# Two gate stages that scale and squash both halves of a block before the rest, and narrow weights loaded into a small tile

## The chip, the cores and the metric

The kernel runs on one core of a Trainium2 chip. The metric is the device time of one execution in microseconds (us); below 0.2% (5.6 us) two versions of it cannot be told apart.

## The reference

Two model blocks run one after the other over 1024 positions of width 1024, batch 1, in float32. The first has two layers, one with windowed attention and one with latent attention (`mla`), and each layer ends in a gate; the second has a state-space branch and an attention branch behind one wide projection. What the change touches is, cut to its core:

```python
# first block, per layer i (0: windowed attention, 1: mla)
h = h + y
gate = jax.nn.sigmoid(rms_norm(h, ple_norm_g[i]) @ ple_w_gate[i])     # 1024 x 1024
h = h + (p[i] @ ple_w[i]) * gate
# mla: cq 384 columns, ckv 256, k_rope 32, z 1024
cq, ckv, k_rope, z = jnp.split(u @ w_in, ...)
# second block: ada = silu(c) @ w_ada + b_ada gives shift, scale, gate
h = _rmsnorm(x, norm_w) * (1.0 + scale) + shift
z_ssm, xbc, dt_raw, q, k, v, z_att, f_logit, g_logit = jnp.split(h @ w_in, ...)   # dt_raw 16 columns, f_logit 8
```

## The kernel before, in words

Activations are kept transposed: 8 tiles (k = 0 to 7) of 128 channels by 1024 positions, worked on in two halves of 512 positions. To keep float32 accuracy each operand is split into a high and a low part, and a product takes three matmuls (`mm3`: L148, L149, L150). An output block of 128 channels costs 24 matmuls per half. Its weights come in on a DMA into a raw tile (`wr`, 2 buffers), ScalarE makes the high part (L107), VectorE the low part (L108). Every tile is taken from a ring with a fixed number of buffers: `wr`, `wh`, `wl` have 2, `T` (128x512, for scratch) has 4, `P` has 4, PSUM has two double-half tiles `S` and three single-half `TR`. A new tile waits until the old one in its buffer has been read for the last time.

**The gate, `ple`.** Each block n = 0 to 7 is multiplied and then evacuated half by half: VectorE multiplies PSUM by the norm's factor into a `T` tile (L438), ScalarE applies tanh (L754), VectorE multiplies by the projected embedding (L755) and adds into h (L756), and `nxt` then prepares the next stage: in layer 0 the split of the new h (L88 on ScalarE, L89 on VectorE) and its squares (L311 on ScalarE, L325 on GpSimd, summed over positions by one-column matmuls, L335); in layer 1 the squares of two norms. Layer 0 calls `lin`, which computes both halves and then evacuates both. Layer 1 calls `lin1`: first all blocks of half 0, then of half 1; between them the second norm's factor is worked out, and pieces of `second_in` (L1087 to L1090) are slipped in.

**The ada steps.** In layer 0 each gate block is followed by two steps of `ada_steps`: a 512 KB DMA of a row block of w_adaT into a `P` tile (L1051) and one VectorE reduction over it (L1053).

**Narrow weights, `stacked`.** The 32 columns of k_rope (`mla_in`) and the 16+16 columns for dt and f (`ssd_in`) are loaded into a raw tile (L124), and their high and low parts (L126 on ScalarE, L127 on VectorE) stand side by side in one `wh` tile; `mm2` (L134) multiplies both at once, 16 matmuls per half. In `mla_in` they come after the ckv blocks, in `ssd_in` directly after the last gate block.

The order within each engine's queue is not the order of the code: a scheduler in the framework places the instructions by its own estimates before the kernel is built. At run time each engine works through its queue strictly in that order, so an instruction that waits holds up all that stand behind it.

Of the kernel before, what the change touches and what calls it, by code (L numbers as in the profile page):

```python
# [17 lines left out]
ALU = mybir.AluOpType  # L18
AX = mybir.AxisListType

P = 128
T = 1024
NB = 8
# [15 lines left out]
class Kern:  # L39
# [79 lines left out]
    def stacked(self, srcs):  # L119

        nc = self.nc
        raw = self.t("wr", (P, NB, 32))
        for c, s in srcs:
            nc.sync.dma_start(raw[:, :, c:c + s.shape[1]], s.rearrange("(k p) n -> p k n", p=P))  # L124
        w = self.t("wh", (P, NB, 64), F32R)
        nc.scalar.activation(w[:, :, 0:32], raw, AF.Copy)  # L126
        nc.vector.tensor_tensor(w[:, :, 32:64], raw, w[:, :, 0:32].bitcast(F32), op=ALU.subtract)  # L127
        return w
# [22 lines left out]

    def lin(self, w, x, evac, cut=0, tag="S"):

        if tag == "S":
            ps = self.ps("S", (P, 2, HT))
            ps = [ps[:, half, :] for half in range(2)]
        else:
            ps = [self.ps(tag) for _ in range(2)]
        for k0, k1 in ((0, cut), (cut, len(x))):
            if k0 < k1:  # L160
                for half in range(2):
                    self.mm3(ps[half], w, x, half, k0, k1)
        for half in range(2):
            evac(half, ps[half])

    def lin1(self, w, x, half, evac, tag=None):

# [576 lines left out]
    def ple(self, i, hs, xs, rb, nxt, side):  # L744

        nc = self.nc
        wg = self.A["ple_w_gate"][i]
        pwd = self.pwd

        def evac(n, pw, off):  # L750
            def ev(half, ps):
                sl = slice(half * HT, half * HT + HT)
                t = self.scaled(ps, rb, half)
                nc.scalar.activation(t, t, AF.Tanh, scale=0.5)  # L754
                nc.vector.scalar_tensor_tensor(t, t, 1.0, pw[:, sl] if off is None else pw, op0=ALU.add, op1=ALU.mult)  # L755
                nc.vector.scalar_tensor_tensor(hs[n][:, sl], t, 0.5, hs[n][:, sl], op0=ALU.mult, op1=ALU.add)  # L756
                nxt(n, half, hs[n][:, sl])
            return ev
        if i == 0:
            for n in range(NB):  # L760
                pw = self.t("P")
                nc.sync.dma_start(pw, pwd[n])
                self.lin(self.weights([(0, wg[:, n * P:n * P + P])], NB), xs, evac(n, pw, None), CUT if n == 0 else 0)
                next(side)
                next(side)
            return
        for half in range(2):
            for n in range(NB):
                pw = self.t("P", (P, HT))
                nc.sync.dma_start(pw, pwd[n, :, half * HT:half * HT + HT])  # L770
                self.lin1(self.weights([(0, wg[:, n * P:n * P + P])], NB), xs, half, evac(n, pw, half))
                for _ in range(0 if half == 0 else (1, 1, 1, 2, 2, 2, 0, 0)[n]):
                    next(side)

# [1026 lines left out]
```

## Time and profile before

| what | us |
|---|---|
| median of 3 runs (2803.79 to 2805.35) | 2805.26 |
| the profiled execution, its own time | 2801.53 |
| its span | 2799.8 |
| TensorE (PE) busy | 2730.1 |
| VectorE (DVE) busy | 1614.5 |
| ScalarE (ACT) busy | 1317.6 |
| GpSimd (POOL) busy | 964.1 |

A timeline row gives the start, the duration, the engine, the line, the operation and its tiles, and at its end the time the engine had been idle and whose end let it go. SPq is the queue of DMA issues; its rows are the issue, not the transfer. PEclk is the granted TensorE clock, 1.00 for 2.4 GHz and 0.50 for 1.2 GHz. A row marked x2 or x8 holds that many instructions. A 512-column matmul lasts 0.39 us but starts 0.23 us after the one ahead of it, so 24 take 5.5 us. The gate of layer 0 runs from 527 to 612 us, `mla_in`'s narrow weights stand at 665, the gate of layer 1 runs from 1414 to 1517, and `ssd_in` starts there.

### The profile page before, as it was taken

The numbers are of one execution on the slowest core, as the hardware profiler recorded it, in microseconds if no ns is written. First come the engines' busy times: TensorE is split into PE (matmuls) and PEld (weight loads), VectorE is DVE, ScalarE is ACT, GpSimd is POOL, SyncE is SP. The second block draws the span as 40 slices with busy tenths as digits, with TensorE's granted clock in tenths as the row PEclk, the third lists the DMA queues.
The fourth block names the chain that finished last, engine by engine and source line by source line (L and its number), as shares of the span: only waits on it lengthen the run. The fifth ranks groups of instructions, "written<-read, shape, count | busy, mean of one in ns | idle before, by whom it ended". The sixth has DMA issues, their size and how long they took to land.

```text
span 2799.8 us, 37840 instructions
## 1 busy us (share of the span) xinstructions
PE 2730.1 (98%) x13951; PEld 2248.3 (80%) x13951; DVE 1614.5 (58%) x2981; ACT 1317.6 (47%) x2520; POOL 964.1 (34%) x802
## 2 busy tenths in 40 slices
PE   8999989999999999999998999999999999999998
PEld 6888778878888888888876777777888888888877
DVE  6786864565478778876467674564322332323364
ACT  5675663333267777786344444532133333334231
POOL 2333352112145555553234113221144444543031
PEclk9999999999999999999999999999999999999999
DMA  4011034452431111112344111223411111112442
GB/s 141 24 31 46 26 106 158 123 170 52 107 80 34 34 34 39 48 44 81 109 136 133 31 54 50 76 83 106 136 46 46 38 46 38 46 50 91 132 140 79
DMA packets 249304, 212.89 MB, mean 76 GB/s; under 512 B 35296, under 2 KB 203296, under 8 KB 249120
## 3 DMA queue, kind: packets, MB, share of 16 engines
q1 hardware_dynamic: 249120, 210.49, 25.8%
q8 instruction: 110, 1.80, 0.3%
q14 instruction: 74, 0.61, 0.1%
HBM read 159.03 MB, written 38.44 MB: 71 GB/s over the span
## 4 chain that ended last, share of the span: by engine, by line
PE 80%; DVE 9%; ACT 4%; DMA 3%; issue 3%; POOL 1%; SPq 0%; DVEq 0%; ACTq 0%; POOLq 0%
PE psTR L185 9%; PE psTR L187 9%; PE psTR L186 9%; PE psS L149 8%; PE psS L148 8%; PE psS L150 8%; PE psOV L999 4%; PE psTR L988 3%; PE psS L1692 3%; DMA P<-in_w_adaT 2%; PE psS L969 2%; PE psS L971 2%; PE psS L970 2%; PE psTR L1586 1%; PE psOV L650 1%
## 5 line engine op out<-in xcount | busy, mean ns | idle before, releaser
L86 DVE TENSOR_TENSOR PT<-psTR,PT 128x512 fp32r<-128x512 f32 (+2 forms) x448 | 284.5, 646 | 184.8 <-ACT PT L85 182.1
L107 ACT ACTIVATE wh<-wr 128x1024 fp32r<-128x1024 f32 (+2 forms) x185 | 177.1, 958 | 422.0 <-PE psS L149 295.0
L185 PE MATMUL psTR<-X,wh 128*128 128x512 f32 x864 | 354.1, 410 | 3.6 <-DVE PT L86 3.3
L85 ACT ACTIVATE PT<-psTR 128x512 fp32r<-128x512 f32 (+2 forms) x448 | 246.2, 563 | 221.8 <-PE psTR L1586 137.8
L187 PE MATMUL psTR<-X,wl 128*128 128x512 f32 x864 | 342.7, 397 | 0.0
L186 PE MATMUL psTR<-X,wh 128*128 128x512 f32 x864 | 341.1, 395 | 0.0
L108 POOL TENSOR_TENSOR wl<-wr,wh 128x1024 fp32r<-128x1024 f32 x66 | 159.1, 2410 | 393.0 <-ACT wh L107 392.7
L148 PE MATMUL psS<-X,wh 128*128 128x512 f32 x688 | 271.9, 397 | 11.3 <-ACT wh L107 6.9
L149 PE MATMUL psS<-X,wh 128*128 128x512 f32 x688 | 271.9, 396 | 0.6 <-POOL X L676 0.3
L150 PE MATMUL psS<-X,wl 128*128 128x512 f32 x688 | 271.3, 395 | 0.9 <-DVE wl L108 0.9
L325 POOL TENSOR_TENSOR R<-R,T 128x512 f32<-128x512 f32 x81 | 118.5, 1464 | 411.1 <-ACT T L311 381.6
L999 PE MATMUL psOV<-PT,X 128*128 128x256 f32 x1024 | 188.6, 297 | 8.1 <-DVE PT L86 5.5
L187 PEld LDWEIGHTS psTR<-X,wl 128*128 128x128 f32 x864 | 162.7, 188 | 36.4 <-issue 1.7
L185 PEld LDWEIGHTS psTR<-X,wh 128*128 128x128 f32 x864 | 163.4, 189 | 30.2 <-DVE PT L86 4.0
L186 PEld LDWEIGHTS psTR<-X,wh 128*128 128x128 f32 x864 | 163.5, 189 | 23.4 <-issue 0.8
L953 DVE TENSOR_REDUCE nm<-psS 128x1 f32<-128x1024 f32 x128 | 155.5, 1216 | 20.8 <-PE psS L971 20.2
L148 PE MATMUL psS<-G,wh 128*128 128x512 f32 x400 | 159.4, 399 | 7.4 <-ACT wh L107 4.4
L999 PEld LDWEIGHTS psOV<-PT,X 128*128 128x128 f32 x1024 | 147.8, 189 | 22.4 <-DVE PT L86 7.4
L148 PEld LDWEIGHTS psS<-X,wh 128*128 128x128 f32 x688 | 130.7, 190 | 41.9 <-ACT wh L107 8.6
L150 PE MATMUL psS<-G,wl 128*128 128x512 f32 x400 | 159.9, 400 | 0.2 <-DVE wl L108 0.2
L108 DVE TENSOR_TENSOR wl<-wr,wh 128x1024 fp32r<-128x1024 f32 (+2 forms) x93 | 116.6, 1255 | 74.7 <-ACT wh L107 73.9
L149 PE MATMUL psS<-G,wh 128*128 128x512 f32 x400 | 159.3, 398 | 0.0
(414 smaller groups left out, 6473.5 us busy)
## 6 DMA issues: line engine op xcount, KB each, us to landing
wr<-in_w_in SPq DMA_DIRECT2D x66, 512.0 KB
wr<-in_ple_w_gate SPq DMA_DIRECT2D x24, 512.0 KB
wr<-in_a_w_in SPq DMA_DIRECT2D x16, 512.0 KB
P<-in_w_adaT SPq DMA_DIRECT2D x16, 512.0 KB
gd<-T SPq DMA_DIRECT2D x32, 256.0 KB
T<-gd SPq DMA_DIRECT2D x32, 256.0 KB
wr<-in_b_w_in SPq DMA_DIRECT2D x13, 512.0 KB
X<-X SPq DMA_DIRECT2D x48, 128.0 KB
```

The costliest lines, as they stand in the source:

```text
L85: last = nc.scalar.activation(hi, src, AF.Copy)
L86: (nc.gpsimd if pool else nc.vector).tensor_tensor(lo, src, hi.bitcast(F32), op=ALU.subtract)
L107: self.nc.scalar.activation(hi[:, k, :], raw[:, k, :], AF.Copy)
L108: (self.nc.gpsimd if pool else self.nc.vector).tensor_tensor(lo[:, k, :], raw[:, k, :], hi[:, k, :].bitcast(F32), op=ALU.subtract)
L148: self.nc.tensor.matmul(ps, hi[:, k, :], xh, start=(k == 0), stop=False)
L149: self.nc.tensor.matmul(ps, hi[:, k, :], xl, start=False, stop=False)
L150: self.nc.tensor.matmul(ps, lo[:, k, :], xh, start=False, stop=(k == nk - 1))
L185: nc.tensor.matmul(ps, hi[:, k, :], xh, start=(k == 0), stop=False)
L186: nc.tensor.matmul(ps, hi[:, k, :], xl, start=False, stop=False)
L187: nc.tensor.matmul(ps, lo[:, k, :], xh, start=False, stop=(k == nk - 1))
L953: nc.vector.tensor_reduce(nm, st, axis=AX.X, op=ALU.max, negate=True)
L999: nc.tensor.matmul(po[:, u % 2, :], vt[:, 2 * kk + a, :], pe[:, part, a, :], start=(kk + a == 0 and part == 0), stop=(kk + a == 4 and part ...
```

## The change

The raw tile of `stacked` is taken from the ring `T` instead of `wr`. `lin` collects what `evac` returns and calls it after both halves. In `ple` the evacuation ends with tanh and returns the rest as a function. In layer 0 both halves thus pass L438 and tanh before either passes L755. In layer 1 the evacuation of block 0 of half 0 is held back until block 1's matmuls have been emitted; the other blocks are evacuated as before.

```diff
     def stacked(self, srcs):
-        raw = self.t("wr", (P, NB, 32))
+        raw = self.t("T", (P, NB, 32))
...
     def lin(self, w, x, evac, cut=0, tag="S"):
-        for half in range(2):
-            evac(half, ps[half])
+        late = [evac(half, ps[half]) for half in range(2)]
+        for fn in late:
+            if fn is not None:
+                fn()
...
                 t = self.scaled(ps, rb, half)
                 nc.scalar.activation(t, t, AF.Tanh, scale=0.5)
-                nc.vector.scalar_tensor_tensor(t, t, 1.0, pw[:, sl] if off is None else pw, op0=ALU.add, op1=ALU.mult)
-                nc.vector.scalar_tensor_tensor(hs[n][:, sl], t, 0.5, hs[n][:, sl], op0=ALU.mult, op1=ALU.add)
-                nxt(n, half, hs[n][:, sl])
+
+                def rest():
+                    nc.vector.scalar_tensor_tensor(t, t, 1.0, pw[:, sl] if off is None else pw, op0=ALU.add, op1=ALU.mult)
+                    nc.vector.scalar_tensor_tensor(hs[n][:, sl], t, 0.5, hs[n][:, sl], op0=ALU.mult, op1=ALU.add)
+                    nxt(n, half, hs[n][:, sl])
+                return rest
...
+        rest = []
         for half in range(2):
             for n in range(NB):
...
-                self.lin1(self.weights([(0, wg[:, n * P:n * P + P])], NB), xs, half, evac(n, pw, half))
+                rest.append(self.lin1(self.weights([(0, wg[:, n * P:n * P + P])], NB), xs, half,
+                                      lambda half, ps, ev=evac(n, pw, half): lambda: ev(half, ps)()))
+                if half > 0 or n > 0:
+                    for fn in rest:
+                        fn()
+                    rest.clear()
```

The instructions are the same ones; their places in the queues differ in the gate of layer 0, around the narrow weights in `mla_in`, and from the gate of layer 1 into `ssd_in`. Lines of the changed kernel are numbered 3 higher from `lin` on and 12 higher behind `ple` (L438 is L441, L755 is L760, L1053 is L1065).

In the gate of layer 0 this is one block (the sixth, PSUM tile 5642) in VectorE's queue, before:

```order
L438 TENSOR_TENSOR T_5691<-psS_5642,R_5245 128x512
L108 TENSOR_TENSOR wl_5812<-wr_5810,wh_5811 128x1024
L1053 ISA P_5802,ada_552<-P_5802,P_5275,vec_78 128x1024
L1053 ISA ada_552 128x1
L755 SCALAR_TENSOR_TENSOR T_5691<-T_5691,P_5634 128x512
L756 SCALAR_TENSOR_TENSOR O_4939<-T_5691,O_4939 128x512
L438 TENSOR_TENSOR T_5704<-psS_5642,R_5245 128x512
L89 SCALAR_TENSOR_TENSOR X_5697<-O_4939,vec_78,X_5696 128x512
L1053 ISA P_5805,ada_552<-P_5805,P_5275,vec_78 128x1024
```

and now:

```order
L441 TENSOR_TENSOR T_5691<-psS_5642,R_5245 128x512
L441 TENSOR_TENSOR T_5694<-psS_5642,R_5245 128x512
L1065 ISA P_5802,ada_552<-P_5802,P_5275,vec_78 128x1024
L1065 ISA ada_552 128x1
L108 TENSOR_TENSOR wl_5812<-wr_5810,wh_5811 128x1024
L760 SCALAR_TENSOR_TENSOR T_5691<-T_5691,P_5634 128x512
L760 SCALAR_TENSOR_TENSOR T_5694<-T_5694,P_5634 128x512
L761 SCALAR_TENSOR_TENSOR O_4939<-T_5691,O_4939 128x512
L761 SCALAR_TENSOR_TENSOR O_4939<-T_5694,O_4939 128x512
L1065 ISA P_5805,ada_552<-P_5805,P_5275,vec_78 128x1024
```

The second half's read of PSUM has moved ahead of the reduction over w_adaT; the next weights' low part has moved behind it.

The narrow weights of `mla_in` in the queue of DMA issues, before (`wr_6399` and `wr_6464` are later, wide weights):

```order
L104 DMA wr_6170<-in_b_w_in 128x8x128
L776 DMA h2d<-O_5087 128x512 x2
L104 DMA wr_6237<-in_b_w_in 128x8x128
L124 DMA wr_6337<-in_b_w_in 128x8x32
L104 DMA wr_6399<-in_b_w_in 128x8x128
L104 DMA wr_6464<-in_b_w_qb 128x3x32 x4
```

and now:

```order
L104 DMA wr_6237<-in_b_w_in 128x8x128
L104 DMA wr_6399<-in_b_w_in 128x8x128
L104 DMA wr_6464<-in_b_w_qb 128x3x32 x4
L124 DMA T_6337<-in_b_w_in 128x8x32
L104 DMA wr_6514<-in_b_w_in 128x8x128
```

The load has moved behind two wide ones, and its `T` buffer is that of T_6292, the first half of the last ckv block after its scaling: the load waits until L88, L89 and L311 (now L88, L89, L314) have read that. TensorE's queue puts the eight L335 of that block's norm ahead of the 32 L134, where before they came after.

The narrow weights of `ssd_in` in the same queue, before (`h4d<-O` are the stores of the gate's result, half 1, one per block):

```order
L776 DMA h4d<-O_14003 128x512
L124 DMA wr_15217<-in_w_in 128x8x16 x2
L770 DMA P_15119<-pwd_12758 128x512
L776 DMA h4d<-O_14077 128x512
L104 DMA wr_15225<-in_w_in 128x8x128
L770 DMA P_15164<-pwd_12758 128x512
L104 DMA wr_15233<-in_w_in 128x8x128
L776 DMA h4d<-O_14151 128x512
```

and now:

```order
L104 DMA wr_15241<-in_w_in 128x8x128
L777 DMA P_15164<-pwd_12758 128x512
L788 DMA h4d<-O_14151 128x512
L104 DMA wr_15600<-in_w_in 128x8x128
L788 DMA h4d<-O_14225 128x512
L788 DMA h4d<-O_14299 128x512
L124 DMA T_15217<-in_w_in 128x8x16 x2
L104 DMA wr_15666<-in_w_in 128x8x128
```

The load has moved from the fourth of the eight blocks' stores to behind the last; its buffer is that of the squares of block 6, whose last reader is GpSimd's addition (L328, before L325). On ScalarE and VectorE L126 and L127 now stand behind everything of block 7. TensorE's queue still has the 16 L134 next after the last gate block, then the 16 L338 (before L335) and then the first conv block; before, the conv block's matmuls stood between them.

At the middle of layer 1's gate TensorE's queue before had L335 directly behind block 0 of half 1, then blocks 1 and 2; now it has block 2, the L338, and blocks 1, 4, 3. Weights for block 2 take the buffer that block 0 frees, weights for block 4 that of block 1.

## Rows read from the trace of the kernel before

**Rows 1.** The page, parts 1 and 4: busy time by engine, and the chain.

```profile
PE 2730.1 (98%) x13951; PEld 2248.3 (80%) x13951; DVE 1614.5 (58%) x2981; ACT 1317.6 (47%) x2520; POOL 964.1 (34%) x802
...
PE 80%; DVE 9%; ACT 4%; DMA 3%; issue 3%; POOL 1%; SPq 0%; DVEq 0%; ACTq 0%; POOLq 0%
```

**Rows 2.** Windows: length, then PE, PEld, DVE, ACT, POOL busy, PEclk, DMA share, GB/s.

```profile
500.00:620.00 120.00, 113.25 (x497) 90.31 (x496) 79.89 (x118) 42.37 (x64) 22.06 (x16) 1.00 0.52 158
...
1440.00:1480.00 40.00, 36.07 (x151) 29.14 (x150) 30.44 (x53) 17.75 (x26) 18.58 (x14) 0.91 0.55 171
...
1517.00:1574.00 57.00, 51.72 (x219) 39.13 (x219) 35.64 (x69) 25.23 (x38) 20.63 (x14) 0.88 0.27 74
...
1472.30:1479.10 6.80, 6.80 (x24) 5.93 (x24) 5.79 (x30) 1.42 (x3) 0.73 (x1) 0.50 0.39 117
...
1523.50:1530.30 6.80, 4.57 (x10) 2.82 (x11) 5.54 (x8) 3.20 (x5) 0.42 (x1) 0.50 0.37 92
```

**Rows 3.** Timeline of TensorE, gate of layer 0: two of five gaps.

```profile
588.36 0.47 PE L148 MATMUL psS<-G,wh 128*128 128x512 f32 x1 [1.30 <-ACT X L88]
...
612.75 0.50 PE L148 MATMUL psS<-X,wh 128*128 128x512 f32 x1 [2.35 <-ACT X L88]
```

**Rows 4.** Timeline of VectorE, gate of layer 0.

```profile
587.53 0.68 DVE L438 TENSOR_TENSOR T<-psS,R 128x512 f32<-128x512 f32 x1
...
591.43 1.28 DVE L1053 CUSTOM_DVE_ANT_0 P<-P,P,vec 128x1024 f32<-128x1024 f32 x1 [2.27 <-DMA P<-in_w_adaT]
```

**Rows 5.** Timeline of the DMA queue, gate of layer 0.

```profile
580.45 0.33 SPq L1051 DMA_DIRECT2D P<-in_w_adaT  x1
...
586.31 0.33 SPq L1051 DMA_DIRECT2D P<-in_w_adaT  x1
...
593.35 0.33 SPq L1051 DMA_DIRECT2D P<-in_w_adaT  x1
```

**Rows 6.** Timelines of PE, ACT and POOL around mla_in's narrow weights.

```profile
664.87 7.53 PE L134 MATMUL psS<-X,wh 128*64 128x512 f32 x32
...
672.92 1.84 PE L335 MATMUL psTR<-ones,R 128*128 128x1 f32 x16
...
653.97 0.42 ACT L126 ACTIVATE wh<-wr 128x256 fp32r<-128x256 f32 x1 [10.57 <-PE psS L149]
...
665.86 0.71 ACT L88 ACTIVATE G<-T,vec 128x512 fp32r<-128x512 f32 x1
...
667.22 3.14 POOL L325 TENSOR_TENSOR R<-R,T 128x512 f32<-128x512 f32 x2 [21.90 <-ACT T L311]
```

**Rows 7.** Timelines of the DMA queue and POOL: two 64 KB moves and their reader.

```profile
675.78 1.22 SPq L812 DMA_DIRECT2D P<-P  x2
...
679.03 3.25 POOL L813 TENSOR_TENSOR P<-P,PT 32x1024 f32<-32x1024 f32 x1 [8.67 <-DMA P<-P]
```

**Rows 8.** Timelines of PE, ACT and DVE at the middle of layer 1's gate.

```profile
1471.86 1.52 PE L335 MATMUL psTR<-ones,R 128*128 128x1 f32 x8 [3.88 <-POOL R L325]
...
1470.92 1.04 ACT L107 ACTIVATE wh<-wr 128x1024 fp32r<-128x1024 f32 x1
...
1471.99 2.12 DVE L108 TENSOR_TENSOR wl<-wr,wh 128x1024 fp32r<-128x1024 f32 x1 [1.65 <-ACT wh L107]
```

**Rows 9.** Timelines of PE, DVE and POOL, end of the gate and ssd_in.

```profile
1516.84 0.40 PE L150 MATMUL psTR<-G,wl 128*128 128x512 f32 x1
1517.83 2.06 PE L134 MATMUL psTR<-G,wh 128*64 128x512 f32 x8 [0.60 <-DVE wh L127]
...
1525.49 0.79 PE L148 MATMUL psS<-G,wh 128*128 128x512 f32 x1 [4.44 <-ACT wh L107]
...
1574.21 0.40 PE L148 MATMUL psS<-G,wh 128*128 128x512 f32 x1
...
1517.37 0.41 DVE L127 TENSOR_TENSOR wh<-wr,wh 128x256 fp32r<-128x256 f32 x1
...
1532.46 1.74 POOL L325 TENSOR_TENSOR P<-P,T 128x512 f32<-128x512 f32 x1
```

## The prediction

> **What bounds the kernel now.** I read the page first: TensorE (PE) is busy 2730.1 of 2799.8 us and makes up 80% of the chain [rows 1]. So a shorter or longer evacuation counts only where PE stands still for it, or where PE runs at the lower clock. Then windows over the stages that the change touches [rows 2]: in the gate of layer 0 (500 to 620 us) PE is idle 120 - 113.25 = 6.75 us at full clock; from 1440 to 1480, the middle of layer 1's gate, 3.9 us at a mean clock of 0.91; from 1517 to 1574, where ssd_in begins, 5.3 us at 0.88. Last the timelines at these gaps, to see who lets PE go [rows 3 to 9]. About 16 us of idle time and some clock loss is all that any reordering here can win; but PE has no slack, so a wait put into its way is paid in full.
>
> One feature of the clock matters for each wait. After 3.88 us of idle at 1471.86 [rows 8] the granted clock is 0.50 for at least 6.8 us [rows 2]; in the gate of layer 0, whose longest gap is 2.35 us [rows 3], it stays 1.00 [rows 2]. So I charge a stall of 3.5 us or more another 3.4 us (half of 6.8), and one of 2.5 us nothing.
>
> **The gate of layer 0.** Before, PE's start at 588.36 waits [rows 3] for the PSUM tile of two blocks earlier, whose second half L438 reads at 587.53 [rows 4]. (The row names L88, which was long done; L438's end fits.) That L438 stands behind a reduction L1053 which waits for its w_adaT load: issue 586.31, start of the reduction 591.43, thus 5.12 us, after DVE had waited 2.27 [rows 4, 5]. The loads are serial, since each waits for the reduction before it: issues at 580.45, 586.31 and 593.35, 6.45 us each, 12.9 a block, against 11.0 for the block's 48 matmuls at 0.23. So DVE falls behind PE and hands PSUM back late; that is the 6.75 us.
>
> Now L438 of both halves stand ahead of the reduction. The second half's read comes one load earlier (6.4 us) less the 0.7 of its new neighbours, more than the largest gap, so the gaps between blocks go. The loads stay serial; one issue in two no longer has the embedding's load ahead of it and saves 0.6. What takes the gaps' place: L108 of a later block now stands behind the reduction, and would come up to 0.9 late at one block (I take 0.4); the first block of mla_in still wants the split of the last gate block, where the 2.35 gap stood, for which I take 1.2; and 0.4 for the squares. Sum 6.75 - 2.0 = 4.7 saved. Bounds: 6.75, all of it, and 1.5, if the loads pace the weights instead.
>
> **Narrow weights in mla_in.** Before, they lay ready: L126 ran at 653.97 and the 32 L134 at 664.87, with no gap [rows 6]. Now the load waits for the buffer of the ckv block that PE has only just finished at 665.1. Readers of that buffer: L88 at 665.86 for 0.71, then L89 and L311, about 667.3 in all; the load goes out then. The time from issue to use of a 128 KB load in 128-byte pieces stands in no row. Below, two moves of 64 KB each are issued from 675.78 for 1.22 and read at 679.03, so 2.6 us after the last issue [rows 7]; above, 512 KB takes 5.1 [rows 4, 5]. I take 3.0, near the 64 KB row. Then L126 0.42 and L127 0.41 with 0.2 for hand-over: L134 starts at 671.3 instead of 665.1, 6.2 us later. In that gap PE can do the eight L338, whose additions end on POOL at 670.4 [rows 6], worth 1.7 us (672.92 to 674.6 before). Left 4.5 idle, and 3.4 for the clock: 7.9 lost. Bounds: with 2.6 and no clock loss 4.1; with 5.1 and a longer low clock 11.5.
>
> The Trainium skill (DMA: Bandwidth & Descriptors, Anatomy of one DMA) puts a transfer at 2.0 us plus bytes over 436 GB/s, fitted for another issuing engine; an estimate by it is 2.3 us here, and the sum would be 0.7 us smaller at this place and at the next. The rows above, which include the queue, are longer, and I go by them.
>
> **The gate of layer 1.** At its start one more wait for the broadcast of the norm's factor, hidden before behind block 1: 0.3 lost. In the middle, L335 waited 3.88 us for POOL's sum of block 7, with 3.4 for the clock, together 7.3. Now block 2 comes first. Its weights take the buffer that PE has just freed: L107 1.04 and then L108, 2.12 beside POOL's additions [rows 8]; two matmuls run in between, so 2.5 idle. The same once more at block 4, whose weights take block 1's buffer and whose L108 stands third in DVE's queue: 2.6. So 2.2 saved, if neither lowers the clock; bounds 0 and 7.
>
> **Narrow weights in ssd_in.** This is the largest term. Before, PE ends the gate at 1517.1 and starts L134 at 1517.83, as L127 has run at 1517.37 [rows 9]. Now the load waits for POOL's second addition of block 6, which before ended at 1532.46 + 1.74 = 1534.2, 17.1 us after PE's end, because a block's tail passes DVE, ACT and POOL in turn and these are that far behind PE. In the new order one L108 is done earlier and L127 and another L108 later, but PE also ends earlier, so I take 15 us. Then 3.3 for two issues and landing, 0.42 and 0.41 for L126 and L127, 0.2: PE idle for 19.3 us. The L338 that stand next can't run ahead in an ordered queue, nor the conv block behind them. Then the same work as before with one stretch of low clock (3.4) and 1.0 for waits on the second half's activations: 23.7 lost. Before, the losses of this stretch were 0.7 + 5.3 idle, and 0.88 of mean clock over 57 us is 13.7 us at half speed, of which PE was busy 11.4 (2.2 of idle lies in the window at 1523.5 [rows 2]), so 5.7: 11.7 in all. Net 12 lost. Bounds: 4, if POOL is only 8 us behind; 18 with 5.1 for the landing, a longer low clock and POOL as late as before.
>
> **Sum.** -4.7 + 7.9 + 0.3 - 2.2 + 12 = +13.3 us on the profiled execution of 2801.53 (span 2799.8), so 2814.8. The median of the runs, 2805.26, is 3.7 above that execution: 2818.5. A fifth of a percent, 5.6 us, is what a measurement of this kernel can tell from no change.
>
> **Rivals.**
> First, faster: the narrow load hides. `T` turns over in a ring of four, so if its buffer fell free 5 us before PE came, both loads would be covered as before and only the gates' gains stay: -4.7 + 0.3 - 2.2, and up to 4 more where ssd_in's stall of 4.44 [rows 9] shrinks because the wide weights no longer share `wr` with it: 2795 to 2799. It decides at the end of POOL's addition against PE's end of the gate; the trace has that addition 17 us late, and mla_in's buffer is freed only by the block that PE has just finished. 0.08. The Trainium skill (Trainium Kernel Development and Optimization, Best Practices) says to double-buffer so that DMA overlaps compute; by that rule four buffers would give this rival. The trace speaks against it, as the ring here is held by the evacuation itself.
>
> Second, a draw: the gates give all they can (6.75 and 7) and the narrow loads cost their lower bounds (4.1 and about 6): -3.7, 2801 to 2809. For it: the scheduler put the work so by its own estimates. Against: two bounds at once. 0.13.
>
> Third, the loads pace the gate: layer 0 saves 1.5, layer 1 nothing, the two waits take 11.5 and 16: +26, 2831. For it: the serial loads are no fewer than before, and DVE's L108 took 2.12 beside POOL [rows 8]. 0.10.
>
> Fourth, the reordering of halves brings nothing because PE's gaps in layer 0 come from the split L88, as the row says, and not from PSUM: then +4.7 more than forecast, 2823, within the range. 0.09.
>
> **How the numbers follow.** The forecast has 0.60 with its own range of 2811 to 2825. Out to the draw and towards the third rival, 2804 to 2829 holds 8 in 10. Faster by over 5.6 us: the first rival and a part of the draw, 0.10. Within 5.6 us (to 2811): the rest of the draw and the forecast's low end, 0.13. Slower: 0.77.
>
> **What would show it.** In the profile after: no gaps over 1 us between gate blocks of layer 0, with two L441 in a row on DVE; TensorE idle some 5 us just before L134 at about 665, ended by L127, and the granted clock at 0.50 behind it; two gaps of about 2.5 us after block 0 of half 1; and one gap of 15 to 22 us ahead of L134 at the end of the gate, with the load L124 issued when POOL's addition of block 6 ends. The prediction is wrong if that last gap is under 8 us, if L124 is issued before PE ends the gate, or if layer 0 keeps its gaps.

## The result, and the profile after

The changed kernel takes 2830.22 us (median of 4 runs, 2829.02 to 2832.63) against 2805.31 us for the kernel before, run beside it: a ratio of 1.0085, interval 1.0069 to 1.0101. It is slower, as forecast, but by 24.9 us where 13.3 were forecast. That is 5.2 us above the forecast's own range (2811 to 2825) and 1.2 above the wider one (2804 to 2829). The profiled execution took 2829.53 us (span 2827.5). Its page, part 1:

```profile
PE 2732.4 (97%) x13951; PEld 2247.7 (79%) x13951; DVE 1611.8 (57%) x2981; ACT 1317.6 (47%) x2520; POOL 969.6 (34%) x802
```

TensorE has the same 13951 matmuls and 2.3 us more of busy time than before [rows 1]; the loss is waiting. Windows of the same profile, in the columns of [rows 2]:

```profile
500.00:620.00 120.00, 114.53 (x501) 90.88 (x501) 80.18 (x120) 42.27 (x64) 24.51 (x17) 1.00 0.51 161
620.00:720.00 100.00, 95.77 (x420) 76.44 (x419) 47.94 (x91) 26.40 (x40) 15.96 (x8) 0.97 0.24 57
...
1480.00:1520.00 40.00, 37.92 (x156) 30.27 (x157) 23.67 (x49) 14.53 (x20) 14.14 (x10) 0.91 0.38 118
1520.00:1540.00 20.00, 6.88 (x29) 4.99 (x27) 15.31 (x21) 9.58 (x14) 15.35 (x11) 0.79 0.35 108
1540.00:1600.00 60.00, 48.64 (x222) 37.38 (x223) 32.25 (x63) 22.39 (x35) 15.71 (x11) 0.87 0.17 46
```

In the gate of layer 0, 5.47 us of idle time are left of 6.75. Around mla_in TensorE is idle 4.2 us, and from 1520 to 1600 some 24.5 us. Because both programs have the same number of matmuls, the start of one with the same number can be compared in both traces. So read, the gate of layer 0 gained 1.0 us, mla_in lost 7.6, the gate of layer 1 lost 2.6 (0.8 won up to the change of halves, 3.4 lost behind it) and ssd_in lost 14.6. That makes 23.8. The spans of the two profiles differ by 27.7; the remaining 3.9 are scatter of up to 2 us a stage, in stages far from the change.

TensorE's waits in the gate of layer 0, from the timeline (start, duration; in brackets the idle time before, and what ended it):

```profile
577.18 0.50 PE L150 MATMUL psS<-G,wl 128*128 128x512 f32 x1 [1.17 <-DVE wl L108]
589.24 0.50 PE L150 MATMUL psS<-G,wl 128*128 128x512 f32 x1 [0.62 <-DVE wl L108]
602.20 0.50 PE L150 MATMUL psS<-X,wl 128*128 128x512 f32 x1 [1.52 <-DVE wl L108]
611.88 0.50 PE L150 MATMUL psS<-X,wl 128*128 128x512 f32 x1 [0.34 <-DVE wl L108]
614.44 0.50 PE L148 MATMUL psS<-X,wh 128*128 128x512 f32 x1 [1.83 <-ACT X L88]
```

The gaps of [rows 3] stood ahead of L148 and were put down to PSUM; four of these five stand ahead of L150, which wants the low part of the weights, and end with its split, L108. VectorE in the same stretch:

```profile
596.27 1.27 DVE L441 TENSOR_TENSOR T<-psS,R 128x512 f32<-128x512 f32 x2
599.71 1.28 DVE L1065 CUSTOM_DVE_ANT_0 P<-P,P,vec 128x1024 f32<-128x1024 f32 x1 [2.17 <-DMA P<-in_w_adaT]
...
600.92 1.22 DVE L108 TENSOR_TENSOR wl<-wr,wh 128x1024 fp32r<-128x1024 f32 x1
```

The DMA queue there ("x2" is a row of two issues, from the start of the first to the end of the second):

```profile
580.95 7.46 SPq L1063 DMA_DIRECT2D P<-in_w_adaT  x2
...
592.97 8.39 SPq L1063 DMA_DIRECT2D P<-in_w_adaT  x2
```

The two L441 do stand together, and PSUM is free early. But the reduction (L1053 before, L1065 now) waits 2.17 us for its load, and the weight split L108 stands behind it; L150 at 602.20 starts when L108 ends. A pair of loads still takes 12.0 us (580.95 to 592.97), a block of matmuls 11.0.

The end of layer 1's gate and ssd_in, which [rows 9] show of before. TensorE's timeline:

```profile
1527.30 0.40 PE L150 MATMUL psTR<-G,wl 128*128 128x512 f32 x1
1551.36 3.67 PE L134 MATMUL psTR<-G,wh 128*64 128x512 f32 x8 [23.66 <-DVE wh L127]
```

GpSimd's last row in this stretch, the second addition for block 6's square sums:

```profile
1544.16 1.71 POOL L328 TENSOR_TENSOR P<-P,T 128x512 f32<-128x512 f32 x1
```

VectorE's last addition into h, of block 7:

```profile
1544.78 1.63 DVE L761 SCALAR_TENSOR_TENSOR O<-T,O 128x512 f32<-128x512 f32 x1
```

The DMA queue, with the stores of blocks 6 and 7 and then the narrow load:

```profile
1542.15 4.61 SPq L788 DMA_DIRECT2D h4d<-O  x2
1546.85 1.14 SPq L124 DMA_DIRECT2D T<-in_w_in  x2
```

ScalarE, the high part:

```profile
1550.43 0.42 ACT L126 ACTIVATE wh<-T 128x256 fp32r<-128x256 f32 x1 [2.75 <-DMA T<-in_w_in]
```

VectorE, the low part:

```profile
1550.88 0.42 DVE L127 TENSOR_TENSOR wh<-T,wh 128x256 fp32r<-128x256 f32 x1 [4.47 <-ACT wh L126]
```

This is the forecast chain with one link more. The addition L328 frees the buffer of T at 1545.87. But the store of block 7 stands ahead of the load in the DMA queue and waits for L761, which ends at 1546.41; the load L124 goes out behind it at 1546.85. Its data are used at 1550.43, and L127 lets TensorE go.

### The profile page after: what moved, and what is told of

The parts are those of the page before. It is cut to its first block, busy times and chain, and to the rows that moved or that the text cites. A ratio compares the mean times of both kernels' runs of the same rounds, so it can differ in the third digit from the quotient of the medians.

```text
span 2827.5 us, 37847 instructions
## 1 busy us (share of the span) xinstructions
PE 2732.4 (97%) x13951; PEld 2247.7 (79%) x13951; DVE 1611.8 (57%) x2981; ACT 1317.6 (47%) x2520; POOL 969.6 (34%) x802
## 4 chain that ended last, share of the span: by engine, by line
PE 79%; DVE 9%; ACT 4%; DMA 3%; issue 3%; POOL 1%; SPq 0%; DVEq 0%; ACTq 0%; POOLq 0%
PE psTR L188 9%; PE psTR L189 9%; PE psTR L190 9%; PE psS L150 8%; PE psS L149 8%; PE psS L148 8%; PE psOV L1011 4%; PE psTR L1000 3%; PE psS L1704 3%; PE psS L983 2%; PE psS L981 2%; PE psS L982 2%; DMA P<-in_w_adaT 1%; PE psTR L1598 1%; PE psOV L653 1%
## 5 line engine op out<-in xcount | busy, mean ns | idle before, releaser
L107 ACT ACTIVATE wh<-wr 128x1024 fp32r<-128x1024 f32 (+2 forms) x185 | 177.1, 957 | 428.6 <-PE psS L149 289.8
L108 POOL TENSOR_TENSOR wl<-wr,wh 128x1024 fp32r<-128x1024 f32 x66 | 158.6, 2403 | 398.7 <-ACT wh L107 397.6
L148 PE MATMUL psS<-X,wh 128*128 128x512 f32 x688 | 273.2, 398 | 11.1 <-ACT wh L107 8.5
L150 PE MATMUL psS<-X,wl 128*128 128x512 f32 x688 | 272.6, 397 | 5.9 <-DVE wl L108 5.9
L328 POOL TENSOR_TENSOR R<-R,T 128x512 f32<-128x512 f32 x81 | 120.3, 1490 | 406.0 <-ACT T L314 376.4
L148 PEld LDWEIGHTS psS<-X,wh 128*128 128x128 f32 x688 | 131.3, 191 | 43.9 <-ACT wh L107 10.6
L150 PE MATMUL psS<-G,wl 128*128 128x512 f32 x400 | 159.5, 399 | 1.8 <-DVE wl L108 1.8
L150 PEld LDWEIGHTS psS<-X,wl 128*128 128x128 f32 x688 | 131.1, 191 | 36.9 <-DVE wl L108 8.4
L148 PE MATMUL psS<-G,wh 128*128 128x512 f32 x400 | 158.6, 397 | 0.6 <-DVE T L1425 0.5
```

The source lines that it names most:

```text
L107: self.nc.scalar.activation(hi[:, k, :], raw[:, k, :], AF.Copy)
L108: (self.nc.gpsimd if pool else self.nc.vector).tensor_tensor(lo[:, k, :], raw[:, k, :], hi[:, k, :].bitcast(F32), op=ALU.subtract)
L148: self.nc.tensor.matmul(ps, hi[:, k, :], xh, start=(k == 0), stop=False)
L150: self.nc.tensor.matmul(ps, lo[:, k, :], xh, start=False, stop=(k == nk - 1))
```

## The experiments

Two theories stood against each other. By the buffer theory, the late buffer of T for the narrow weights is nearly the whole loss, and holding back evacuations is worth little either way. By the order theory, the held-back evacuations push VectorE and GpSimd back behind the gate, and the load only shows it. All ratios are against the kernel before, run on the same chip.

**Parts of the change alone.** e1 keeps both deferrals and takes the tile from `wr` again (`wr` has two buffers, not four as the expectation says):

```
-        raw = self.t("T", (P, NB, 32))
+        raw = self.t("wr", (P, NB, 32))
```

> Both gate blocks deferred, the narrow weights back in the four-buffer wr tile. Buffer theory (the late T buffer costs +7.7 us in mla_in and +14.6 us in ssd_in, the deferral -1.0 us in gate 0 and +2.7 us in gate 1): 2805.3 + 1.7 = about 2807 us, PE's gap ahead of ssd_in's first narrow matmul back to under 12 us. Order theory (the deferral itself makes VectorE and GpSimd late behind gate 1, and the T buffer only shows it): the gap at ssd_in stays near 20 us and the time is 2818 us or more.

Measured: 2807.82 us, ratio 1.0012 (1.0003 to 1.0021). TensorE's waits at the start of ssd_in are short:

```profile
1524.88 0.68 PE L134 MATMUL psTR<-X,wh 128*64 128x512 f32 x2 [1.39 <-DVE X L1102]
1526.80 0.50 PE L148 MATMUL psS<-G,wh 128*128 128x512 f32 x1 [1.23 <-ACT wh L107]
...
1529.93 0.80 PE L150 MATMUL psS<-G,wl 128*128 128x512 f32 x1 [1.77 <-DVE wl L108]
```

e2 keeps T and takes both deferrals out:

```
-        late = [evac(half, ps[half]) for half in range(2)]
-        for fn in late:
+        for half in range(2):
+            fn = evac(half, ps[half])
...
-                if half > 0 or n > 0:
+                if True:
```

> Only the narrow weights' tile is changed, both gate blocks as they were. Buffer theory: 2805.3 + 7.7 + 14.6 = about 2827.6 us, with PE gaps of about 4.5 us ahead of mla_in and 23 us ahead of ssd_in. Order theory: mla_in's +7.7 us and little of ssd_in's, about 2813 us.

Measured: 2828.19 us, ratio 1.0085 (1.0071 to 1.0099), the whole change's ratio. By matching matmuls, as above, mla_in loses 9.0 us and ssd_in 12.6. The gaps:

```profile
668.18 3.57 PE L338 MATMUL psTR<-ones,R 128*128 128x1 f32 x16 [3.46 <-POOL R L328]
...
1548.49 3.35 PE L134 MATMUL psTR<-G,wh 128*64 128x512 f32 x8 [20.72 <-DVE wh L127]
```

The order theory falls: without any deferral the gap at ssd_in is 20.7 us. What lets the load go can be read here too. The addition for block 6 on GpSimd:

```profile
1539.46 1.27 POOL L328 TENSOR_TENSOR P<-P,T 128x512 f32<-128x512 f32 x1
```

The DMA queue, with the store of block 7 and the load behind it:

```profile
1543.17 0.32 SPq L788 DMA_DIRECT2D h4d<-O  x1
1543.58 1.14 SPq L124 DMA_DIRECT2D T<-in_w_in  x2
```

The buffer of T is free at 1540.73, and the load goes out 2.85 us later, when the store ahead of it has gone. So T makes the load late in two ways: by its buffer, and by the late place that the load has in the queue. Here it is the place that sets the start.

e3 and e4 have one deferral each (the first or the second half of that diff left out) and `wr`.

> Only layer 0's gate blocks are deferred, the narrow weights in wr. From the trace of the changed kernel, gate 0 gains 1.0 us (the weight split of L108 now waits behind the reduction that the w_adaT loads pace): 2804 us, with PE gaps of 0.6 to 1.8 us between the blocks that VectorE's L108 ends. The prediction's own term (4.7 us gained): 2800.6 us.

Measured: 2804.34 us, 1.0002 (0.9993 to 1.0011). The deferral in layer 0 makes no difference that can be measured. Its gate window has 115.09 us of busy TensorE, against 115.57 for e4, which has no deferral there. The windows, of e3:

```profile
500.00:620.00 120.00, 115.09 (x499) 91.48 (x497) 80.00 (x118) 42.28 (x64) 24.81 (x17) 0.99 0.50 161
```

and of e4:

```profile
500.00:620.00 120.00, 115.57 (x502) 92.38 (x501) 81.55 (x126) 42.36 (x64) 22.05 (x16) 0.99 0.51 158
```

So even the 1.0 us read above is within what one profile of this gate differs from another: by matching matmuls, the gate is 0.8 to 2.2 us shorter than before in e2, e4 and f3 too, which have no deferral there.

> Only the first block of layer 1's gate is deferred, the narrow weights in wr. From the trace of the changed kernel: +2.7 us by gate 1's end and nothing behind it, 2808 us, with stalls on the weights of the first blocks of half 1 and two stretches of half clock. The prediction's own term (2.2 us gained): 2803 us. Order theory: the gap ahead of ssd_in grows as well, 2815 us or more.

Measured: 2805.68 us, 1.0007 (0.9998 to 1.0016); by matching matmuls the gate loses 2.2 us (0.8 won up to the change of halves, 3.0 lost behind it) and ssd_in 1.8. The prediction's gain of 2.2 is not there, nor a growth of the gap at ssd_in to the size that the order theory wanted.

**Is it the ring, or the tile's place in the queues?** f4 is the changed kernel with the narrow weights in a tile that lies idle (the two mask tables that live there later are loaded behind it); f3 does the same without deferrals.

```
-        raw = self.t("T", (P, NB, 32))
+        raw = self.t("tables", (P, NB, 32))
```

> The changed kernel with one edit: the narrow weights' raw tile in the idle tables tile in place of T, both deferrals kept. Ring theory: both narrow waits go (-7.7 and -14.6 us) and the deferral's +2 to +4 us stay: 2803 to 2809 us. If the deferral's own order had put the narrow load behind GpSimd's and VectorE's tails, 2820 us or more.

Measured: 2805.03 us, 1.0007 (0.9998 to 1.0016). This edit gives back 0.78 of the 0.85%. The DMA queue shows why: this is ssd_in's load,

```profile
658.09 0.99 SPq L124 DMA_DIRECT2D tables<-in_w_in  x2
```

issued 860 us ahead of its use, and the narrow matmuls at mla_in (first row) and ssd_in (second) start without a wait:

```profile
667.12 7.53 PE L134 MATMUL psS<-X,wh 128*64 128x512 f32 x32
...
1523.69 1.98 PE L134 MATMUL psTR<-G,wh 128*64 128x512 f32 x8
```

The edit takes the load out of the ring and, with that, to a far earlier place in the queue. It shows what T costs, not which of the two holds the load.

> The order of before (no deferral); the narrow weights' raw tile is neither in wr nor in T but in the single tables tile, which is idle at both places (the triangular masks are loaded into it later). Ring theory (a wait for the ring's buffer is the whole cost, and wr as the narrow tile delays the wide loads): no loss in mla_in, and ssd_in's stall of 4.4 us on the wide weights with its stretch of half clock shrinks: 2797 to 2802 us. If it was the narrow tile's place in the queues and not the ring, ssd_in keeps a loss of over 8 us beside before: 2813 us or more.

Measured: 2802.53 us, 0.9998 (0.9990 to 1.0007). No loss, but not the gain either: the stall of 4.4 us on L107 [rows 9] goes, and the next one takes its place, on the activations of the second norm:

```profile
1525.46 1.11 PE L134 MATMUL psTR<-X,wh 128*64 128x512 f32 x2 [3.89 <-DVE X L1102]
```

g2 leaves T in place and lightens GpSimd behind the gate (the edit moves this instruction in both halves, not only in the first as the expectation says):

```
-                nc.gpsimd.tensor_scalar(t, t, gp[:, k:k + 1], ada[:, k:k + 1], op0=ALU.mult, op1=ALU.add)
+                nc.scalar.activation(t, t, AF.Identity, scale=gp[:, k:k + 1], bias=ada[:, k:k + 1])
```

> The changed kernel with one edit: the eight scale-and-shift instructions of the second norm's first half (L1101 in the changed kernel, about 1.26 us each between 1507 and 1539 us) run on ScalarE instead of GpSimd. If the turn of the T ring sets the narrow load's start, and GpSimd's and VectorE's work behind the gate sets that turn, block 6's additions end 2 to 6 us sooner against PE's end of the gate, the load follows them, and the gap of 23.7 us shrinks by as much: 2824 to 2828 us. If the gap is made of landing and queue order, it stays within 1 us: 2830 us.

Measured: 2824.29 us, 1.0079 (1.0064 to 1.0094); by time alone it can't be told from the changed kernel. Its timelines can. TensorE:

```profile
1546.37 3.68 PE L134 MATMUL psTR<-G,wh 128*64 128x512 f32 x8 [19.88 <-DVE wh L127]
```

GpSimd's last addition:

```profile
1539.38 1.71 POOL L328 TENSOR_TENSOR P<-P,T 128x512 f32<-128x512 f32 x1
```

The DMA queue:

```profile
1542.07 1.14 SPq L124 DMA_DIRECT2D T<-in_w_in  x2
```

The addition ends at 1541.09, 15.0 us behind the start of the gate's last matmul (1526.09), where it was 18.6 in the changed kernel (1527.30 to 1545.87). The load again goes out 0.98 us after it, and the gap is 3.8 us shorter. So the work of VectorE and GpSimd behind the gate sets when the load goes out. The addition and the L761 ahead of the store (it ends at 1541.63 here) moved together, so g2 can't part the ring from the queue. Of those 3.8 us ssd_in kept only 0.4, since the clock stayed low longer behind the gap (last section).

**What paces the gate of layer 0?** f1 has before's order and f2 the deferral of layer 0; in both the loads are left out and the reduction takes the resident `cb`:

```
-            nc.sync.dma_start(raw, self.A["w_adaT"][n * P:n * P + P, :])
...
-                nc.vector.tensor_tensor_reduce(out=raw, in0=raw, in1=cb, scale=0.5, scalar=self.v("b_ada_2", n),
+                nc.vector.tensor_tensor_reduce(out=raw, in0=cb, in1=cb, scale=0.001, scalar=self.v("b_ada_2", n),
```

> The order of before (no deferral, narrow weights in wr), but the 16 w_adaT loads are left out: the reductions run over the resident cb instead, so layer 1's modulation is other data. If the serial loads alone make VectorE late in gate 0, the PE gaps of 6.75 us go although the second halves' reads still stand behind the reductions: about -6 us there, and about 2799 us. If the order of the halves or the split L88 makes the gaps, they stay: 2805 us.

> Gate 0 deferred, narrow weights in wr, the 16 w_adaT loads left out in the same way. If the loads pace the gate, the gaps on the weight split L108 (3 of 0.7 to 1.3 us) and on L88 go here as well and gate 0 ends within 0.5 us of the undeferred kernel without loads: 2799 us. If the deferral has a gain of its own that L108 behind the reduction had eaten, gate 0 is 3 us or more shorter than there.

Measured: 0.9982 (0.9973 to 0.9991) for f1 and 0.9979 (0.9969 to 0.9988) for f2. The gate's window, of f1:

```profile
500.00:620.00 120.00, 120.00 (x533) 97.42 (x532) 86.82 (x132) 42.40 (x64) 23.28 (x16) 1.00 0.36 111
```

and of f2:

```profile
500.00:620.00 120.00, 120.00 (x533) 97.45 (x532) 86.79 (x133) 42.90 (x65) 27.60 (x17) 1.00 0.36 117
```

TensorE has no gap in either order, and by matching matmuls the gate is 8.2 us shorter in both, of which the ratios keep 5 to 6. The serial loads make all the gaps; the order of the halves only decides at which instruction TensorE meets them. (Without them the DMA share falls as well, from 0.5 to 0.36. That it is the wait for them and not their traffic is read from the 2.17 us above; no run parts the two.)

**A version meant to beat both.** g1 is f3 with 8 of the 16 load-and-reduce steps taken in out_proj, where VectorE has room; g3 adds g2's edit.

```
             self.lin(w, x, ev, CUT if n == 0 else 0)
+            if side is not None:
+                next(side)
...
                 next(side)
-                next(side)
...
+    side = K.ada_steps()
...
-    K.ple(0, hs, xs, rb, nxt, K.ada_steps())
+    K.ple(0, hs, xs, rb, nxt, side)
```

> The order of before, the narrow weights in the idle tables tile, and 8 of the 16 w_adaT steps issued one per block in out_proj of layer 0 and the other 8 one per block in gate 0. If the serial loads are what holds gate 0 back (the kernels without the loads were 0.2% faster in either order), the gaps between its blocks mostly go and 5 to 7 us are won: 2796 to 2799 us. If the early reductions hold up VectorE in out_proj instead, the gaps move there: 2802 to 2806 us.

Measured: 2799.65 us, 0.9985 (0.9975 to 0.9994). The gate again lost its gaps (TensorE busy 120.00 of 120); in out_proj one new wait stands at 463.82, 2.91 us, for an addition that waits for its residual input behind the w_adaT loads:

```profile
463.82 0.47 PE L148 MATMUL psS<-X,wh 128*128 128x512 f32 x1 [2.91 <-DVE O L713]
```

By matching matmuls out_proj loses 3.2 of the 8.2 us that the gate wins. A gain of 0.15% is below the 0.2% by which two versions can be told apart, though the interval lies below 1.

> The kernel with the spread loads and the narrow weights in tables, and the scale-and-shift on ScalarE. ssd_in's stall of 3.9 us that X (L1102) ends in the tables kernel should shrink, as VectorE and GpSimd no longer share those pieces: 2792 to 2797 us. If ScalarE becomes late for the weight copies L107 instead, 2799 us or more.

Measured: 2797.19 us, 0.9978 (0.9969 to 0.9987), the fastest kernel here that keeps all the loads, just past the 0.2%; its interval overlaps with g1's. The stall of 3.89 us is gone. TensorE's two longest waits in ssd_in are now one on the wide weights and, later, one on the second norm:

```profile
1520.67 0.76 PE L148 MATMUL psS<-G,wh 128*128 128x512 f32 x1 [1.28 <-ACT wh L107]
...
1543.19 2.05 PE L293 MATMUL psTR<-T,ones 128*128 128x512 f32 x2 [3.10 <-DVE r L1107]
```

So a wait of 3.10 has come where one of 3.89 went. The profile is of the slowest of ten executions (2802.00 us), and what g3 gains over g1, if anything, can't be read from it.

## Why the prediction was right or wrong

**Narrow weights in mla_in: the number right, in part by luck.** 7.9 forecast, 7.6 measured. The load went out when forecast (667.3). The DMA queue:

```profile
667.50 0.37 SPq L124 DMA_DIRECT2D T<-in_b_w_in  x1
```

ScalarE:

```profile
670.03 0.42 ACT L126 ACTIVATE wh<-T 128x256 fp32r<-128x256 f32 x1 [1.82 <-DMA T<-in_b_w_in]
```

VectorE:

```profile
670.48 0.43 DVE L127 TENSOR_TENSOR wh<-T,wh 128x256 fp32r<-128x256 f32 x1 [1.46 <-ACT wh L126]
```

TensorE:

```profile
668.53 3.58 PE L338 MATMUL psTR<-ones,R 128*128 128x1 f32 x16 [3.45 <-POOL R L328]
671.97 8.85 PE L134 MATMUL psS<-X,wh 128*64 128x512 f32 x32
```

The window behind the gap, in the columns of [rows 2]:

```profile
668.00:674.80 6.80, 6.27 (x23) 5.04 (x24) 4.45 (x15) 1.58 (x3) 2.15 (x2) 0.50 0.25 47
```

The low clock is as forecast, but the wait is another. The prediction has 4.5 us of idle time, ended by L127, with "the eight L338" inside it. There are sixteen, they stand ahead of L134, and the gap of 3.45 ends when GpSimd's addition lets them go. At the low clock they take until 671.97; L127 has been done since 670.91, and L134 starts without a wait. Without them in its way it could have started at about 671, so the load and the L338 cost nearly the same here; no run parts them.

The load took 2.53 us from issue to use, where 3.0 were taken from the 64 KB row. The estimate of 2.3 us by the Trainium skill (DMA: Bandwidth & Descriptors, Anatomy of one DMA), which the prediction set aside, was nearer: the trace agrees with it to 0.23 us here. At ssd_in the same time, from the end of the two issues (1547.99) to L126, is 2.44.

**Narrow weights in ssd_in: mechanism right but for one link, size short.** 12 forecast, 14.6 measured; 12.6 in e2, without the deferrals. The gap alone is 23.66 where 19.3 were forecast. The step that was mis-sized is "so I take 15 us" for the addition's lag behind TensorE's end: it is 18.3 (1545.87 less 1527.30 and the last matmul's own 0.23). Another 0.98 (2.85 in e2) was not in the sum at all: the load stands behind the store of block 7 in the DMA queue, so it didn't go out when its own buffer fell free. Behind the gap, an estimate from the matched starts and the prediction's 11.7 for before, some 2.5 us were lost where 4.4 were taken; so the net came nearer than the gap did. The rival that four buffers hide the load is refuted by e2, and f4 shows why: the idle tile, with one buffer, lets the load go early and hides it, and the ring of four, which the evacuation holds, doesn't. So the Trainium skill's rule to double-buffer that DMA may overlap compute (Trainium Kernel Development and Optimization, Best Practices) isn't borne out here by a count of buffers: gap 23.66 us with four, none with one.

**The gate of layer 0: wrong.** 4.7 gained was forecast; the runs show nothing that can be told from zero (e3). The failed step is "L108 of a later block now stands behind the reduction, and would come up to 0.9 late at one block (I take 0.4)": L150 came late behind it at four blocks, by 0.34 to 1.52, and by 3.65 in all; and L148 at 614.44 waited 1.83 where 1.2 were taken. So layer 0 kept its gaps, which the prediction had named as a sign of being wrong. The prediction had the reason in its own numbers, loads of 12.9 us a block against 11.0 of matmuls, but treated it as one that delays PSUM. f1 and f2 show that a rate was missing: VectorE has to wait for the loads somewhere in each block, and what it does behind them is late, whichever it is. That the loads pace the gate was the third rival (0.10). Its time, 2831, came out too, but by luck: it has 11.5 and 16 for the two narrow loads, which cost 7.6 and 14.6, and no loss in layer 1. The fourth rival (0.09) had the right size, nothing gained, and the wrong cause: f1 still has the split L88, and no gap.

**The gate of layer 1: no gain.** Forecast 0.3 lost at its start and 2.2 gained in the middle; in the traces 0.8 won up to the change of halves and 3.4 lost behind it, 2.6 lost in all (2.2 in e4). Traces without this deferral lose up to 1.6 behind the change of halves too (f1), so a part of the loss can be scatter. TensorE at the change of halves, after:

```profile
1476.76 0.49 PE L148 MATMUL psS<-X,wh 128*128 128x512 f32 x1 [1.70 <-ACT wh L107]
...
1479.92 0.50 PE L150 MATMUL psS<-X,wl 128*128 128x512 f32 x1 [2.43 <-DVE wl L108]
...
1494.81 0.50 PE L148 MATMUL psS<-X,wh 128*128 128x512 f32 x1 [0.68 <-ACT wh L107]
...
1496.94 0.50 PE L150 MATMUL psS<-X,wl 128*128 128x512 f32 x1 [1.40 <-DVE wl L108]
```

The wait for GpSimd's sum [rows 8] went, as forecast, and two stalls on the weights came. Each has two parts, for the high and for the low weights: 4.1 us where 2.5 were taken, and 2.1 for 2.6. The step "if neither lowers the clock" failed: the window from 1480 has a mean clock of 0.91, so 7.2 of its 40 us ran at half speed, or 3.6 us lost, about as much as before [rows 2]. That the split of the weights had been hidden before behind the wait it replaced is read from the two timelines; no run took it away by itself.

**Sum.** On the terms of the forecast: gate 0 missed by 3.7 to 4.7, gate 1 by 4.5, ssd_in by 2.6, mla_in by -0.3. That is 10.5 to 11.5 of the 11.6 by which the loss was forecast too small. e2 gives the same ratio as the whole change, so the deferrals add nothing that this measurement can tell, while the narrow tile is nearly all of the loss.

## What to carry to other kernels

A load is hidden by a buffer that is free early, not by the number of buffers in its ring: look up who reads the ring's oldest buffer last, and how far behind TensorE that reader runs. Then look at what stands ahead of the load in its queue, and what that waits for. Where a serial chain of loads is slower than the matmuls beside it, moving instructions on the waiting engine only changes who is late; spread the chain over a longer stretch, and see where its waits turn up (g1's gate lost its gaps, and out_proj gave 3.2 us of that back). And when a stall is to go, look at what it had been hiding, and charge that in full.

## What the hardware showed besides

The clock fell without any wait in between. In g2, TensorE works without a gap from 1546.37 on, and these are its windows:

```profile
1547.00:1554.00 7.00, 7.00 (x34) 4.69 (x32) 1.06 (x1) 0.68 (x1) 0.00 (x0) 0.73 0.27 77
1554.00:1561.20 7.20, 7.20 (x26) 6.31 (x27) 3.56 (x28) 0.00 (x0) 0.00 (x0) 0.53 0.00 0
1561.20:1597.00 35.80, 35.80 (x159) 27.62 (x158) 18.46 (x25) 20.96 (x32) 0.00 (x0) 1.00 0.11 30
```

The clock had come back in the first of them, and fell to half (1.2 of 2.4 GHz) again from about 1554.3 on, for 6.8 us. What ran before that were the single-column matmuls L338, from 1552.15. In the changed kernel the same matmuls run from 1556.95, and the clock stays up behind them:

```profile
1559.00:1566.00 7.00, 7.00 (x39) 5.86 (x38) 3.40 (x27) 0.00 (x0) 0.00 (x0) 1.00 0.00 0
```

In e2 it fell too, behind the same matmuls (0.50 from 1559 to 1560). Why it falls there and not here stays open. What it means is that a gap shortened by 3.8 us gave back 0.4.
